# One class of eight PSUM banks, and one ring of SBUF buffers for attention scores, in a one-core NSA and mLSTM step

## The chip, the cores and the metric

The kernel runs on one core of a Trainium2 chip. The metric is the device time of one execution in microseconds (us). The kernel before took 1055.37 us, the median of three runs (1055.33 to 1056.41). TensorE (PE) does the matrix products and writes only to PSUM, which has eight banks of 128 x 512 fp32 values; VectorE (DVE), ScalarE (ACT) and GpSimd (POOL) do the rest, and SyncE (SP) issues nearly all transfers.

## The reference

One inference step through a trunk of two layers, for a prompt of 512 new tokens and for 8 samples of one new token each with 1024 past tokens. Width 1024, fp32.

```python
x <- x + Mixer_i(RMSNorm_i(x));   out = W_out( mix(...) * silu(z) )
# layer 0: native sparse attention, 16 heads of 64 on 4 KV heads
q, kv, win, gates, z = nsa_project(h, w_in)
kc, vc, c_end = compress_branch(kv[:, :, 0:2], pe, w1, b1, w2)   # blocks of 32 rows, stride 16
o = gates[0]*o_c + gates[1]*o_s + gates[2]*o_w                   # compressed, selected, window
# layer 1: mLSTM, 4 heads of 512, chunkwise recurrence
xm, z = split(h @ w_in); c = silu(conv(xm)); q, k from c, v from xm (blocks of 4)
S = (q k^T) * exp(D - mt);  num = S v + decay * q C;  hc = num / max(|den|, exp(-mt))
C = carry_decay * C + k^T (w * v)
out = (rmsnorm(hc) * norm_w + skip * c) * silu(z) @ w_out
```

A final RMSNorm follows. The outputs are both activations, the new cache rows, the window, and the mLSTM states (`C`, `n`, `m` and the convolution's last rows) of the prompt and of the samples.

## The kernel before

Activations stand transposed: features on the 128 partitions, the 520 tokens in two column halves of 260. Every fp32 product is made of three matmuls on parts rounded to the PE's fp32r format: `mm3` (L598) adds whi·xhi, whi·xlo and wlo·xhi into one PSUM tile. Each weight tile is loaded (`wraw`), copied by ACT (`whi`), and subtracted by POOL or DVE (`wlo`); constant strings such as LO_Q choose the engine.

The stages run in this order: norm and the compression of the cache pages, the K/V projection with its tiles turned into natural order (`VNEW`, `VC`, `VT`, `kct`), the query projection (`qr`, `qst`), attention of the prompt (about 300 to 468 us) with the decode work laced in, the output projection, the mLSTM's input projection (`xm`, with the block diagonals `bd` made by DVE), the recurrence with the samples' states `cs` streaming through, the mLSTM's output projection (`uh`, `ul`, added from `mm` into `x` by DVE), and at the end the final norm and the last tiles of the prompt's `C` (`pk`, `kwh`, `kwl`, `pc`, `cpt`, L2739 and on).

All calls to the engines are recorded, and then replayed in orders written out by hand (the tables ORDER and CALLS). So what sets the order on every engine is a list, and it is the same in both kernels. What the pools decide is where a tile lies, and through that which earlier readers an instruction has to wait for. Since all calls are replayed from one line, all instructions have line L504, and the profile is read by the names of the tiles.

PSUM is one pool with four tags: `mm` (2 banks, projections), `s` (3 banks: scores, sums, some transposes), `t` (2 banks, transposes and small products) and `d` (1 bank, decode). A tile of a tag takes the bank of that tag that was let go first in program order. The program has 671 PSUM tiles: 244 of `mm`, 213 of `t`, 180 of `s`, 34 of `d`.

In attention each unit takes score tiles of `s` in PSUM (`s<-KA,qst` and `s<-KB,qst`, two matmuls that add into one tile), DVE writes them with the distance term into an SBUF tile also named `s` (L1471, 7 buffers), ACT takes the exponential, PE turns it, and ACT or DVE copies the turned probabilities to `pt` (L1508, 8 buffers), which the product with V reads. Both SBUF tiles are 128 x 512 fp32.

The decode scores (`dec_qk`, L1163) put a `d` tile into `D["dst"]`, which is read by the add behind it.

Of the kernel before, what the change touches and what calls it, by code (L numbers as in the profile page):

```python
# [9 lines left out]
F32 = mybir.dt.float32  # L10
# [34 lines left out]
SBUFS = 7  # L45
PTB = 8
# [494 lines left out]
def step_kernel(ctx, tc, ap):  # L541
    nc = tc.nc
    R = Rec()
    V, S, G, PE, SP = (Engine(R, n, e) for n, e in (("DVE", nc.vector), ("ACT", nc.scalar), ("POOL", nc.gpsimd),
                                                    ("PE", nc.tensor), ("SP", nc.sync)))
    NE = {"DVE": V, "ACT": S, "POOL": G, "PE": PE, "SP": SP}

    def pool_of(stack, **k):
        return Pool(R, stack.enter_context(tc.tile_pool(**k)), k["bufs"])
# [8 lines left out]
    wp = pool_of(wctx, name="wstream", bufs=2, side="right")  # L558
    ps = pool_of(ctx, name="ps", bufs=1, space=PSUM)

    def bank(tag, bufs, name=None):
        return ps.tile([128, 512], F32, name=name or tag, tag=tag, bufs=bufs)

    def mm_cols(out, lhsT, rhs):
        for c in range(4):
# [1 line left out]
            PE.matmul(out[r], lhsT[:, r], rhs, start=True, stop=True)  # L567

    def mmb():
        return bank("mm", 2)  # L570

    def sb():
        return bank("s", 3)

    def xb():
        return bank("t", 2)

    def db():
        return bank("d", 1)

    cst = const.tile([128, CONSTS.shape[1]], F32, name="cst")
    pt = const.tile([1, 2, 64], I32, name="pt")
# [88 lines left out]
    def rms_close(c, acc, pool):  # L671
        pss = sb()
        PE.matmul(pss[:, :CH], ones, acc, start=True, stop=True)
        rms_factor(pss, pool, rr[c])
# [107 lines left out]
    def cmp_unit(b, c, xp=None):  # L782

        po = sb()
        pw = po[:, 0:256].rearrange("p (h t) -> p h t", h=4)
        raw = cw.tile([128, 2080], F32, name="praw", tag="praw", bufs=3)[:, 0:2048].rearrange("p (g f) -> p g f", g=8)
# [59 lines left out]
    def cmp_second():  # L846

        while second:
            b, c, hs = second.pop(0)
            pk = xb()  # L850
            PE.matmul(pk[:, 0:256], w2[:, c].rearrange("p a d -> p (a d)"), hs.rearrange("p h t -> p (h t)"),
                      start=True, stop=True)
            dst = KC if c == 0 else VT0
            pv = pk[:, 0:256].rearrange("p (a b t) -> p a b t", a=2, b=2)
            for h2 in range(2):
                r = slice(64 * h2, 64 * h2 + 64)
                V.tensor_copy(dst[r, :, b], pv[r, :, h2])
# [4 lines left out]
    def kv_tile(i):  # L862
        w = wkv[i]
        t = cw.tile([128, NTOK], F32, name="kvt", tag="kvt", bufs=3)
        kvt[i] = t
        for c in range(2):
            po = {(0, 1): db, (1, 1): xb, (2, 0): xb}.get((i, c), mmb)()
            for kt in range(8):
                mm3(po[:, :CH], w[0][:, kt], w[1][:, kt], hhi[c][:, kt], hlo[c][:, kt], kt == 0, kt == 7)
                if i == 0:  # L870
                    R.cut()
            V.tensor_mul(t[:, c * CH:(c + 1) * CH], po[:, :CH], rr[c])
        S.dma_start(ap["o_kv"][i], t)
        return t
# [113 lines left out]
    b = 2  # L988
    for i in range(12):
        br, hp = divmod(i, 2)  # L990
# [3 lines left out]
        t = kv_tile(i)  # L994
# [39 lines left out]
    QZ = d1.tile([128, 2, 8, 32], F32, name="QZ")  # L1034
    G.memset(QZ, 0.0)

    PS = d1.tile([128, 1536], F32, name="dPS")
# [54 lines left out]
    D = {}  # L1092
# [70 lines left out]
    def dec_qk(P, u, due):  # L1163

        t, dst = D["dk", u], Tile_("d")

        def run():
            D["dst"] = db()
            kt = D["dk_", u].rearrange("p b (h t) -> p b h t", h=2)
            for par in (1, 0):  # L1170
                for hp in range(2):
                    for cg in (3, 2, 1, 0):
                        b = 2 * cg + par
                        PE.matmul(D["dst"][32 * cg:32 * cg + 32, 0:128], QZ[:, hp, b], kt[:, b, hp],
                                  start=par == 1 and hp == 0, stop=par == 0 and hp == 1)

        def add():
            V.tensor_add(PS[:, u * 128:(u + 1) * 128], PS[:, u * 128:(u + 1) * 128], D["dst"][:, 0:128])
        P.op("PE", 1.3, due, run, r=[t], new=[dst])
        P.op("DVE", 0.2, due + 1.3, add, r=[dst], w=[("PS", u)])  # L1180

# [223 lines left out]
    for k in range(8):  # L1405
# [3 lines left out]
        if k in (3, 5, 7):  # L1409
            u = k // 2 - 1  # L1410
# [9 lines left out]
    at = pool_of(actx, name="att", bufs=3, side="right")  # L1420
# [7 lines left out]
    def att_unit(P, hp, g, i, due):  # L1428
        n = 128 * (i + 1)
        mn, sm = Tile_("mn"), Tile_("sm")  # L1430
        X = {}
# [12 lines left out]
        def part(kind, key):  # L1444
            gk, o = where[key]
            return X[kind, gk][:, o:o + n]
        for gk, ks in enumerate(groups):
            pt_, st = Tile_("s"), Tile_("sx")
            st_.append(st)

            def prod(gk=gk, ks=ks):
                q = qst[hp, g]
                p = X["p", gk] = sb()
                for h2 in sorted({x[1] for x in ks}):
                    kh, brs = 2 * hp + h2, [x[0] for x in ks if x[1] == h2]
                    o = where[brs[0], h2][1]
                    for m, K in enumerate((KA, KB)):
                        if len(brs) == 2:
                            rhs = K[:, kh].rearrange("p (b n) -> p b n", b=2)[:, :, 0:n]
                            out = p[:, o:o + 2 * n].rearrange("p (b n) -> p b n", b=2)  # L1460
                        else:
                            rhs, out = K[:, kh, brs[0] * 512:brs[0] * 512 + n], p[:, o:o + n]
                        PE.matmul(out, q[:, h2, i * 128:(i + 1) * 128], rhs, start=m == 0, stop=m == 1)

            def dist(gk=gk, key=None):
                br, h2 = key
                if key == (0, 0):
                    X["mn"] = at.tile([128, 2, 2], F32, name="mn", tag="mn")
                    X["sm"] = at.tile([128, 2, 2], F32, name="sm", tag="sm")
                if ("s", gk) not in X:  # L1470
                    X["s", gk] = at.tile([128, 512], F32, name="s", tag="s", bufs=SBUFS)  # L1471
                V.tensor_tensor_reduce(part("s", key), part("p", key), D0[:, 384 - 128 * i:512], SLOPES[4 * (2 * hp + h2) + g],
                                       CLAMP, op0=OP.add, op1=OP.min, accum_out=X["mn"][:, h2, br:br + 1])

            def ex(key):
                br, h2 = key
                s = part("s", key)
                S.activation(s, s, AF.Exp, scale=-1.0, bias=X["mn"][:, h2, br:br + 1],
                             accum_out=X["sm"][:, h2, br:br + 1])
            P.op("PE", TA[n], due, prod, r=[D["q", hp, g]], new=[pt_])  # L1480
            for m, key in enumerate(ks):
                f0 = key == (0, 0)
                P.op("DVE", TT[n], due, lambda gk=gk, key=key: dist(gk, key), r=[pt_] + ([] if f0 else [mn]),
                     w=[(mn, key)] + ([(st, key)] if m else []), new=([] if m else [st]) + ([mn, sm] if f0 else []))
                P.op("ACT", TE[n], due, lambda key=key: ex(key), r=[(mn, key)], w=[(st, key), (sm, key)])
# [7 lines left out]
        for gk, ks in enumerate(groups):  # L1493
            h2 = ks[-1][1]
            st, pb_, pt_ = st_[gk], Tile_("s" if h2 else "t"), Tile_("pt")
            pts.append(pt_)

            def scale(key):
                s = part("s", key)
                V.tensor_scalar(s, s, X["sm"][:, key[1], key[0]:key[0] + 1], None, op0=OP.mult)  # L1500

            def tr(gk=gk, m=len(ks) * (i + 1), h2=h2):
                X["pp", gk] = sb() if h2 else xb()
                for j in range(m):
                    PE.transpose(X["pp", gk][:, j * 128:(j + 1) * 128], X["s", gk][:, j * 128:(j + 1) * 128], ident)

            def copy(gk=gk, m=n * len(ks), h2=h2):
                X["pt", gk] = at.tile([128, 512], F32, name="pt", tag="pt", bufs=PTB)  # L1508
                if PTC[2 * i + h2] == "S":
                    S.activation(X["pt", gk][:, 0:m], X["pp", gk][:, 0:m], AF.Copy)  # L1510
                else:
                    V.tensor_copy(X["pt", gk][:, 0:m], X["pp", gk][:, 0:m])
            for key in ks:
                P.op("DVE", TS[n], b_, lambda key=key: scale(key), r=[sm], w=[(st, key)])
            P.op("PE", 0.11 * (i + 1) * len(ks) + 0.02, b_, tr, r=[(st, key) for key in ks], new=[pb_])
            P.op("ACT" if PTC[2 * i + h2] == "S" else "DVE", TC[n], b_, copy, r=[pb_], new=[pt_])
# [22 lines left out]
        u, o = Tile_("u"), Tile_("qo")  # L1539
# [418 lines left out]
    sp = pool_of(sctx, name="st", bufs=1)  # L1958
# [731 lines left out]
    at = 3 + QP0 * 4  # L2690
# [175 lines left out]
```

## Time and profile before

| | before |
|---|---|
| median of 3 runs | 1055.37 us |
| the profiled execution, in all | 1052.93 us |
| its span, first to last instruction | 1051.2 us |
| mean granted TensorE clock | 0.995 |
| DMA, whole span | 197.19 MB, mean 188 GB/s |

How to read it: the profile is of one execution. Busy times of engines overlap; an engine at 97% can still be waited for by others and wait itself. In the page's 40 equal slices of the span PE shows 9 tenths or more in all but three: 7 in the first, and 8 in the 29th (736 to 762 us) and the last. A row of the timeline gives the start, the length, the engine, the line, the operation, what is written and read, partitions x elements, and in brackets how long the engine stood idle just before and what ended that. The busiest single groups are the three matmuls of the projections:

```profile
L504 PE MATMUL mm<-hhi,whi 128*128 128x260 f32 (+1 forms) x952 | 273.9, 288 | 2.2 <-DVE xm L504 1.3
L504 PE MATMUL mm<-hhi,wlo 128*128 128x260 f32 (+1 forms) x952 | 270.4, 284 | 1.0 <-POOL wlo L504 0.7
L504 PE MATMUL mm<-hlo,whi 128*128 128x260 f32 (+1 forms) x952 | 270.3, 284 | 0.0
```

The columns behind the bar are busy us in all, mean ns of one, and the idle time ahead of them with what ended most of it. The first of each three may open a new tile and so wait for a bank; the other two add to it.

### The profile page before, as it was taken

The page shows a single profiled execution, that of the slowest core. Times are in us where ns is not written, and L with a number is a line of the kernel's source. Part 1 is how long each engine was busy: PE and PEld are TensorE (multiplying, and loading weights), DVE is VectorE, ACT ScalarE, POOL GpSimd, SP SyncE. Part 2 cuts the span into 40 slices and gives each one's busy share as a digit, 9 for nine tenths or more (in the row PEclk, how much of TensorE's full clock was granted, in tenths as well). Part 3 has the DMA queues.
Part 4 walks back from the last instruction along what each step waited for, and adds up shares of the span by engine and source line. Part 5 has one row for each costly group of instructions (what it writes and reads, how often), then busy time and mean ns, then how long its engine had stood idle before and what let it go on. Part 6 is the DMA issues. An engine that isn't in the chain of part 4 may idle for free.

```text
span 1051.2 us, 24005 instructions
## 1 busy us (share of the span) xinstructions
PE 1022.5 (97%) x8743; PEld 909.5 (87%) x8743; DVE 787.8 (75%) x1877; ACT 535.0 (51%) x1230; POOL 393.3 (37%) x430
## 2 busy tenths in 40 slices
PE   7999999999999999999999999999899999999998
PEld 6989999899988877779999998898867688787897
DVE  6877764478468887876877675886477998988875
ACT  5253332532467786651444364566555555563533
POOL 1162333434324546462324442342423234434332
PEclk9999999999999999999999999999999999999999
DMA  7664554123435524547435652787789879889543
GB/s 248 202 192 141 156 155 131 36 96 121 144 106 177 141 81 130 153 142 251 142 111 163 203 162 73 243 302 275 259 277 328 273 267 303 295 293 325 161 134 112
DMA packets 124792, 197.19 MB, mean 188 GB/s; under 512 B 16117, under 2 KB 66166, under 8 KB 124418
## 3 DMA queue, kind: packets, MB, share of 16 engines
q1 hardware_dynamic: 118866, 186.37, 54.8%
q10 hardware_dynamic: 5808, 9.28, 2.5%
q8 instruction: 69, 1.13, 0.5%
q14 instruction: 49, 0.40, 0.1%
HBM read 145.89 MB, written 58.10 MB: 194 GB/s over the span
## 4 chain that ended last, share of the span: by engine, by line
PE 83%; DVE 8%; ACT 3%; issue 2%; DMA 1%; SPq 1%; POOL 0%; DVEq 0%; ACTq 0%; POOLq 0%
PE mm L504 51%; PE s L504 18%; PE t L504 10%; PE d L504 5%; ACT s L504 1%; DVE num L504 1%; DVE s L504 1%; DVE cs L504 1%; SPq L504 1%; DMA dk<-in_cache 1%; DVE x L504 1%; DVE qst L504 1%; DMA nw<-in_norms 1%; DVE wlo L504 0%; ACT pt L504 0%
## 5 line engine op out<-in xcount | busy, mean ns | idle before, releaser
L504 PE MATMUL mm<-hhi,whi 128*128 128x260 f32 (+1 forms) x952 | 273.9, 288 | 2.2 <-DVE xm L504 1.3
L504 PE MATMUL mm<-hhi,wlo 128*128 128x260 f32 (+1 forms) x952 | 270.4, 284 | 1.0 <-POOL wlo L504 0.7
L504 PE MATMUL mm<-hlo,whi 128*128 128x260 f32 (+1 forms) x952 | 270.3, 284 | 0.0
L504 PEld LDWEIGHTS mm<-hhi,whi 128*128 128x128 f32 (+1 forms) x952 | 179.2, 188 | 7.2 <-issue 1.7
L504 PEld LDWEIGHTS mm<-hhi,wlo 128*128 128x128 f32 (+1 forms) x952 | 179.1, 188 | 1.6 <-POOL wlo L504 0.9
L504 PEld LDWEIGHTS mm<-hlo,whi 128*128 128x128 f32 (+1 forms) x952 | 178.9, 188 | 0.8 <-DVE hlo L504 0.3
L504 POOL TENSOR_TENSOR wlo<-wraw,whi 128x1024 fp32r<-128x1024 f32 (+2 forms) x55 | 108.8, 1979 | 159.0 <-DVE whi L504 74.8
L504 DVE SCALAR_TENSOR_TENSOR cs<-t,wk,cs 128x512 f32<-128x512 f32 x128 | 88.6, 742 | 6.0 <-ACT cs L504 3.8
L504 ACT ACTIVATE cs<-cs,SBC 128x1024 f32<-128x1024 f32 x64 | 72.0, 1142 | 13.2 <-PE d L504 12.5
L504 POOL TENSOR_SCALAR s<-s,sm 128x128 f32<-128x128 f32 (+3 forms) x63 | 62.8, 1008 | 41.8 <-DVE sm L504 21.1
L504 ACT ACTIVATE s<-s,mn 128x256 f32<-128x256 f32 (+3 forms) x128 | 70.6, 554 | 14.7 <-DVE mn L504 12.7
L504 PE MATMUL s<-phi,w1h 128*128 128x256 f32 (+1 forms) x256 | 77.0, 301 | 0.0
L504 PE MATMUL s<-plo,w1h 128*128 128x256 f32 (+1 forms) x256 | 74.5, 291 | 2.2 <-DVE plo L504 2.0
L504 PE MATMUL s<-phi,w1l 128*128 128x256 f32 (+1 forms) x256 | 74.0, 289 | 0.0
L504 ACT ACTIVATE whi<-wraw 128x1024 fp32r<-128x1024 f32 (+1 forms) x55 | 48.0, 874 | 45.2 <-PE mm L504 34.6
L504 PE MATMUL mm<-uh,whi 128*128 128x260 f32 x224 | 66.5, 297 | 3.6 <-DVE x L504 3.6
L504 DVE CUSTOM_DVE_ANT_0 s<-s,D 128x256 f32<-128x256 f32 (+3 forms) x128 | 57.7, 486 | 10.4 <-PE s L504 7.7
L504 PE MATMUL mm<-uh,wlo 128*128 128x260 f32 x224 | 63.3, 282 | 0.0
L504 PE MATMUL mm<-ul,whi 128*128 128x260 f32 x224 | 63.2, 282 | 0.0
L504 DVE TENSOR_TENSOR wlo<-wraw,whi 128x1024 fp32r<-128x1024 f32 (+1 forms) x47 | 51.9, 1106 | 3.1 <-ACT whi L504 1.8
L504 PEld LDWEIGHTS s<-plo,w1h 128*128 128x128 f32 x256 | 48.5, 189 | 3.9 <-DVE plo L504 2.5
L504 PEld LDWEIGHTS mm<-uh,whi 128*128 128x128 f32 x224 | 42.2, 188 | 9.2 <-DVE x L504 4.5
(479 smaller groups left out, 2650.2 us busy)
## 6 DMA issues: line engine op xcount, KB each, us to landing
cs<-in_state_C SPq DMA_DIRECT2D x64, 512.0 KB, 6.0
o_cs<-cs SPq DMA_DIRECT2D x64, 512.0 KB, 4.8
praw<-in_cache SPq DMA_DIRECT2D x128, 128.0 KB, 3.3
dk<-in_cache SPq DMA_DIRECT2D x128, 128.0 KB, 2.9
wraw<-in_m_in SPq DMA_DIRECT2D x32, 512.0 KB, 4.2
wraw<-in_m_out SPq DMA_DIRECT2D x32, 256.0 KB, 4.4
wraw<-in_w_kv SPq DMA_DIRECT2D x11, 512.0 KB, 4.7
wraw<-in_w_q SPq DMA_DIRECT2D x8, 512.0 KB, 3.6
```

The costliest lines, as they stand in the source:

```text
L504: return f(*[real(x) for x in a], **{n: real(x) for n, x in k.items()})
```

## The change

The four PSUM tags become one tag of eight banks. The SBUF tiles `s` and `pt` of attention share one tag of 7 + 8 = 15 buffers. The decode score tile is kept under a key of its own for each unit, `D["dst", u]`, since several may now be live. No order, no instruction and no constant is changed; on each engine the two programs have the same rows in the same order (PE 5870, DVE 1684, ACT 930, POOL 341 and SP 865 of them), and only the semaphores that they wait for differ.

```diff
     ps = pool_of(ctx, name="ps", bufs=1, space=PSUM)
-    def bank(tag, bufs, name=None):
-        return ps.tile([128, 512], F32, name=name or tag, tag=tag, bufs=bufs)
+    def bank(name):
+        return ps.tile([128, 512], F32, name=name, tag="bank", bufs=8)
...
     def mmb():
-        return bank("mm", 2)
+        return bank("mm")
     def sb():
-        return bank("s", 3)
+        return bank("s")
     def xb():
-        return bank("t", 2)
+        return bank("t")
     def db():
-        return bank("d", 1)
+        return bank("d")
...
         def run():
-            D["dst"] = db()
+            D["dst", u] = db()
...
-                        PE.matmul(D["dst"][32 * cg:32 * cg + 32, 0:128], QZ[:, hp, b], kt[:, b, hp],
+                        PE.matmul(D["dst", u][32 * cg:32 * cg + 32, 0:128], QZ[:, hp, b], kt[:, b, hp],
...
         def add():
-            V.tensor_add(PS[:, u * 128:(u + 1) * 128], PS[:, u * 128:(u + 1) * 128], D["dst"][:, 0:128])
+            V.tensor_add(PS[:, u * 128:(u + 1) * 128], PS[:, u * 128:(u + 1) * 128], D["dst", u][:, 0:128])
...
-                    X["s", gk] = at.tile([128, 512], F32, name="s", tag="s", bufs=SBUFS)
+                    X["s", gk] = at.tile([128, 512], F32, name="s", tag="sp", bufs=SBUFS + PTB)
...
-                X["pt", gk] = at.tile([128, 512], F32, name="pt", tag="pt", bufs=PTB)
+                X["pt", gk] = at.tile([128, 512], F32, name="pt", tag="sp", bufs=SBUFS + PTB)
```

## Prediction, made before the changed kernel was run

> **What bounds the kernel now.** I read three views in this order: the page's busy times and chain, the waits of TensorE, and then the timeline at each place where one of those waits can be a wait for a PSUM bank.
>
> ```profile
> span 1051.2 us, 24005 instructions
> PE 1022.5 (97%) x8743; PEld 909.5 (87%) x8743; DVE 787.8 (75%) x1877; ACT 535.0 (51%) x1230; POOL 393.3 (37%) x430
> PE 83%; DVE 8%; ACT 3%; issue 2%; DMA 1%; SPq 1%; POOL 0%; DVEq 0%; ACTq 0%; POOLq 0%
> ```
>
> TensorE is busy for 97% of the span and holds 83% of the chain that ended last. So most of the time is matmul work which the change leaves alone: no instruction is added, removed or moved on any engine. Only idle time of PE, or the idle time of what PE waits for, can go. The waits of PE, longest sums first (us in total, times, longest one):
>
> ```profile
> PE s L504 <- ACT sq L504: 5.6, 1, 5.6
> PE mm L504 <- DVE x L504: 3.6, 4, 1.5
> PE t L504 <- DVE pr L504: 2.4, 1, 2.4
> PE s L504 <- DVE plo L504: 2.0, 1, 2.0
> ...
> PE t L504 <- DVE dOS L504: 0.4, 1, 0.4
> ```
>
> Each row has to be sorted into one of two kinds. A matmul that reads what the named instruction wrote waits for **data**: `sq`, `pr`, `plo` are read by the next matmul, and no pool of banks changes that. A matmul that writes a bank which the named instruction has just read out waits for a **bank**: `mm` behind DVE `x` (the add of `mm` into `x`), `t` behind a copy of another `t`, `mm` behind `xm`. Those are what the change is about.
>
> **The change part by part.** Before, the classes `mm`, `s`, `t`, `d` own 2, 3, 2 and 1 banks, so a `t` tile takes the bank of the `t` tile two before it. After, a tile takes the bank that was let go longest ago among all eight. The program text gives the count of tiles: 244 `mm`, 213 `t`, 180 `s`, 34 `d`. A bank that had one or two tiles between its uses now mostly has seven. The number of instructions is unchanged, so the cost is nothing in work; what is worth counting is each bank wait and the next date behind it.
>
> *End of the compression stage, 201–206 us.* Timeline rows (start, length, engine, and in brackets the idle time before it and what ended it):
>
> ```profile
> 200.99 0.28 PE L504 MATMUL t<-cst,kct 128*32 128x128 f32 x1 [0.46 <-DVE VNEW L504]
> 202.55 0.28 PE L504 MATMUL t<-cst,kct 128*32 128x128 f32 x1 [0.90 <-ACT VC L504]
> 203.41 1.22 DVE L504 TENSOR_TENSOR wlo<-wraw,whi 128x1024 fp32r<-128x1024 f32 x1
> 204.02 0.33 PE L504 MATMUL t<-cst,VT 128*128 128x128 f32 x1 [0.42 <-ACT VC L504]
> 206.16 0.42 PE L504 MATMUL mm<-hhi,wlo 128*128 128x260 f32 x1
> ```
>
> The three matmuls read `kct` and `VT`, not `VNEW` or `VC`; they wait for the bank. Idle: 0.46 + 0.90 + 0.42 = 1.78. The next date is the matmul at 206.16, which reads the `wlo` that DVE ends at 203.41 + 1.22 = 204.63: PE can come forward by 206.16 − 204.63 = 1.53 before it meets that. DVE's own queue follows PE a little here, so I take **1.3** (ends 0 and 1.53).
>
> *Attention, 300–468 us.* PE has 3 idle us in this window, of which one bank wait shows by name (0.4, `t` behind `dOS`). Shorter ones sit inside the busy time: the first matmul of a score tile writes a new `s` bank, its twin (same shape, same queries) adds to it.
>
> ```profile
> 300.00:468.00 168.00, 164.83 (x1925) 133.46 (x1919) 136.71 (x525) 123.88 (x381) 89.80 (x98) 1.00 0.49 143
> ...
> L504 PE MATMUL s<-KA,qst 128*128 128x512 f32 x48 | 22.0, 459 | 0.3
> L504 PE MATMUL s<-KB,qst 128*128 128x512 f32 x48 | 19.0, 395 | 0.0
> ```
>
> (The first row gives window, span, and busy time of PE, its weight loads, DVE, ACT and POOL, then clock, DMA share and GB/s; the others mean ns of one.) The first of a pair takes 459 − 395 = 64 ns longer, 48 × 64 = 3.1 us; the 48 narrower pairs can add no more than as much, 6.1 in all. That excess is an upper bound, since a first matmul also follows another kind of work. Lower end 0.4. I take **2.4**: 0.4 by name, and two thirds of the 3.1.
>
> ```profile
> DVE s L504 <- PE s L504: 7.7, 14, 1.5
> ACT pt L504 <- PE s L504: 13.4, 14, 2.1
> ```
>
> These rows say what the *SBUF half* of the change is worth. DVE and ACT, in this window, begin `s` and `pt` when PE has made the scores or the transposes, not when a buffer comes free. With seven and eight buffers the oldest one is long done; a shared ring of fifteen gives nothing to wait less for: **0**, ends −0.3 and +0.3 (the 0.3 by the row of `s<-KA`, the only idle time beside it). If the cover went, a `pt` would wait for a transpose that read an old `s`, which is finished by then on the same PE queue.
>
> *Start of the mLSTM projection, 526–530 us.*
>
> ```profile
> 526.42 2.38 POOL L504 TENSOR_TENSOR wlo<-wraw,whi 128x1024 fp32r<-128x1024 f32 x1 [0.70 <-ACT whi L504]
> 526.46 2.49 DVE L504 TENSOR_TENSOR bd<-cst,wc 128x128 f32<-128x128 f32 x1
> 528.87 0.28 DVE L504 TENSOR_TENSOR bd<-cst,wc 128x128 f32<-128x128 f32 x1
> 529.07 0.42 DVE L504 TENSOR_TENSOR xm<-mm,rr 128x260 f32<-128x260 f32 x1
> 529.54 0.39 PE L504 MATMUL mm<-hhi,whi 128*128 128x260 f32 x1 [1.30 <-DVE xm L504]
> ```
>
> PE waits 1.30 for a bank that `xm` reads late, since DVE was held by a `bd` of 2.49 us beside a POOL subtraction that started 0.04 us before it; the next `bd` of the same shape, without POOL beside it, took 0.28. With six more banks the projection goes on: **1.3** (ends 0 and 1.3). [...]
>
> *Output projection and the recurrence, 760–985 us.*
>
> ```profile
> 868.75 0.39 PE L504 MATMUL mm<-uh,whi 128*128 128x260 f32 x1 [0.62 <-DVE x L504]
> 997.48 0.39 PE L504 MATMUL mm<-uh,whi 128*128 128x260 f32 x1 [1.46 <-DVE x L504]
> 1004.82 0.36 PE L504 MATMUL mm<-uh,whi 128*128 128x260 f32 x1 [1.30 <-DVE x L504]
> ```
>
> The row of waits has four such waits, 3.6 us; three are above, the fourth is 3.6 − 0.62 − 1.46 − 1.30 = 0.22 and lies in this window too. Of 0.62 + 0.22 = 0.84 I take **0.6** (ends 0 and 0.84), since the next instructions are data waits with a few tenths to spare.
>
> *The tail of the mLSTM, 985–1011 us.* The two long ones, 1.46 + 1.30 = 2.76, are not worth their length:
>
> ```profile
> 760.00:985.00 225.00, 222.75 (x1565) 167.35 (x1566) 193.91 (x415) 126.82 (x206) 79.82 (x87) 0.99 0.85 286
> 985.00:1011.00 26.00, 23.24 (x190) 21.86 (x189) 24.78 (x62) 9.32 (x21) 8.19 (x7) 1.00 0.59 185
> ```
>
> In the second row DVE is busy 24.78 of 26 us: DVE is the bound there, and PE waits because DVE reads its banks late. A PE that is let go early meets DVE's next product:
>
> ```profile
> 1008.39 0.51 ACT L504 ACTIVATE uh<-HN 128x8 fp32r<-128x8 f32 x4 [1.17 <-DVE HN L504]
> 1009.49 1.28 POOL L504 TENSOR_TENSOR wlo<-wraw,whi 128x512 fp32r<-128x512 f32 x1 [2.24 <-ACT whi L504]
> 1011.25 0.28 PE L504 MATMUL s<-uh,wlo 128*128 128x260 f32 x1
> ```
>
> DVE `HN` lets ACT go on, ACT's next is the `whi` behind which POOL's `wlo` waits, POOL ends at 1009.49 + 1.28 = 1010.77, and PE reads that `wlo` at 1011.25: 0.48 to spare. I take **0.45** (ends 0 and 2.76).
>
> *The end, 1036–1051 us.* From the chain, and two timeline rows:
>
> ```profile
> 1037.01 0.70 DVE kwl L504
> ...
> 1037.76 3.07 PE t L504 x12
> ...
> 1040.85 0.60 ACT cpt L504
> ...
> 1041.50 5.88 PE t L504 x24
> ...
> 1043.27 0.69 DVE L504 TENSOR_TENSOR kwl<-t,kwh 128x512 fp32r<-128x512 f32 x1
> 1044.87 0.39 PE L504 MATMUL t<-vh,kwl 128*128 128x512 f32 x1
> ```
>
> Here all uses are `t` tiles on two banks. PE stands from 1040.83 until `cpt` has left the bank (1041.50, 0.67), and the twelve at 1037.76 stood behind `kwl` reading another (0.70): 1.4 on the path. The later `kwl` ends at 1043.96 and is read at 1044.87, so PE can come forward by 0.91: **0.9** (ends 0 and 1.4). What is late next is that `kwl`.
>
> Sum: 1.3 + 2.4 + 1.3 + 0.6 + 0.45 + 0.9 = 6.95, say **7.0 us**. The profiled execution took 1052.9 in all, 1.7 of it around its span; it is 2.4 below the median of the three runs, 1055.4. The bank waits are the same program in both, so the sum is taken off the median: 1055.4 − 7.0 = **1048.4**. The terms' own uncertainty, halves of most of them, is about 3 either way: 1045.4 to 1051.4.
>
> **The rivals.**
>
> *All of it pays.* Every named bank wait goes in full, and attention gives its upper bound: 1.78 + 6.1 + 1.30 + 3.6 + 0.7 = 13.5, giving 1041.9. For it: each gap is idle PE on a chain that is PE for 83%. Against: the next dates above (1.53, 0.48, 0.91).
>
> *The advance is absorbed.* PE comes out of each stage early and DVE does not, so that the 985–1011 stretch, DVE-bound, ends when it did; only 0.45 + 0.9 = 1.35 remain, 1054.0. For it: DVE's 24.78 of 26. Against it: ahead of that stretch DVE is busy only 193.91 of 225, and waits for PE:
>
> ```profile
> DVE x L504 <- PE mm L504: 7.8, 11, 2.1
> ```
>
> That row is DVE's, in 760–985. An earlier PE brings DVE's adds forward, and with them the start of the stretch. So it needs DVE to be held in that window by something else (its cs transfers, 0.85 DMA share), which I do not see.
>
> *Slower: stretched instructions are dealt anew.* An engine that runs some us earlier meets POOL's subtractions at other places.
>
> ```profile
> 216.15 2.45 DVE L504 SCALAR_TENSOR_TENSOR qst<-qr,qst 64x260 fp32r<-64x260 f32 x1
> ```
>
> One such meeting costs 2.49 − 0.28 = 2.2 by the two `bd` rows, and the row here shows one in the query projection right behind 206 us, where the first 1.3 us are gained and PE uses `wlo` as it is made. DVE's `qr`, `qst` there free the `mm` banks and feed attention. If five more of these fall on the path than now, they cost 11; 11 − 7 = 4 more than before: 1059.4. It turns to slower from four on (4 × 2.2 = 8.8). Against it: banks now give PE seven tiles of room, which hides a DVE that is 2 us late, and a meeting can go as well as come.
>
> *The change does not do what it says.* If the pool took the bank freed last, waits would grow; the program's tiles, though, take the one freed first. For the SBUF half I hold this rival to be true, at 0.
>
> **How the numbers follow.** Forecast (1045.4 to 1051.4) 0.64; all pays 0.10; absorbed 0.14; slower 0.12. About 0.2%, 2.1 us, is what a measurement of this kernel can tell from no change: 1053.3 to 1057.5. Faster: 0.64 + 0.10 = 0.74; same: 0.14; slower: 0.12. The range takes in the first three cases, with half a us or so above the third: 1041.9 to 1055.5.
>
> **What would show it.** Right: no bracket for `VNEW`, `VC`, `xm` at 201–204 and 529; the waits of PE for DVE `x` down from 3.6 to below 1; in the last 10 us no wait for `cpt`; the same rows for `sq`, `pr`, `plo`. The attention step is right if the KA mean of 459 comes near 440 or below. The tail step is right if 985–1011 shows as much DVE work in as long a time, shifted some 5 us earlier, with a new wait of PE for `wlo` at its end. Wrong: a new long PE wait for POOL `wlo` or DVE `qst` in 206–260, DVE busy time above 787.8 by 5 or more, or a shift of PE that shrinks from stage to stage towards 985.

## The result, and the profile after

| | before | changed |
|---|---|---|
| median of 12 runs each | 1055.35 us | 1047.74 us |
| ratio, 95% interval | | 0.9944 [0.9925, 0.9963] |
| the profiled execution, in all | 1052.93 us | 1046.14 us |
| its span | 1051.2 us | 1044.4 us |
| mean granted TensorE clock | 0.995 | 0.998 |

The time predicted was 1048.4. One of the twelve runs before took 5626.69 us, which a median hardly feels. The page of the changed kernel, its span, busy times and chain:

```profile
span 1044.4 us, 23991 instructions
PE 1017.0 (97%) x8743; PEld 908.3 (87%) x8743; DVE 789.8 (76%) x1877; ACT 534.7 (51%) x1230; POOL 392.8 (38%) x430
PE 78%; DVE 10%; ACT 5%; DMA 3%; issue 2%; SPq 1%; POOL 1%; DVEq 0%; ACTq 0%; POOLq 0%
```

The same work, and PE a smaller part of the chain: where PE used to stand for a bank it now more often stands for a product of another engine. The waits of PE of the changed kernel say which:

```profile
PE s L504 <- ACT sq L504: 5.6, 1, 5.6
PE s L504 <- DVE plo L504: 2.8, 2, 2.0
PE t L504 <- DVE pr L504: 2.3, 1, 2.3
PE mm L504 <- POOL wlo L504: 1.6, 2, 0.8
...
PE t L504 <- DVE hs L504: 1.4, 1, 1.4
PE t L504 <- ACT VT L504: 1.0, 1, 1.0
```

The bank waits (`x` 3.6, `VC` 1.3, `xm` 1.3, `cpt` 0.7, `VNEW` 0.5) are gone, all of them. In their place stand `hs`, `VT` and more `wlo`: data.

One thing has to be taken out before the two traces can be laid side by side. Windows of 1 us of the kernel before (window, span, PE busy, granted clock, DMA share, GB/s):

```profile
203.00:204.00 1.00, 0.60 (x2) 1.00 0.00 0
204.00:205.00 1.00, 0.94 (x5) 0.75 0.10 34
205.00:206.00 1.00, 1.00 (x7) 0.50 0.52 120
206.00:207.00 1.00, 1.00 (x6) 0.50 0.76 178
207.00:208.00 1.00, 1.00 (x7) 0.54 0.81 315
208.00:209.00 1.00, 1.00 (x11) 1.00 0.06 25
```

For 3.4 us PE runs at half clock, which costs 1.7 us where PE has work all the while, as here, and less where it would have waited. The trace of before holds three such stretches (204, 651, 760 us; 5.1 us lost), that of after one (755 us; 1.7 lost): half of the 6.8 us between the two spans. So two measures are used below. *At full clock* is a run's time multiplied by its mean granted clock. The *lead* at a place is the start of a matmul in the trace of before less that of the same matmul in the other trace, both reduced by what the half-clock stretches ahead of it cost.

| lead gained in | forecast | changed | changed, again | psum_only | kb_early |
|---|---|---|---|---|---|
| 0 to 187 us | 0 | -1.5 | -2.5 | -3.2 | -0.7 |
| 187 to 206 us | 1.3 | -0.7 | -0.4 | -0.5 | -0.3 |
| 206 to 300 us | 0 | +0.2 | +0.3 | +0.3 | +0.3 |
| 300 to 470 us, attention | 2.4 | +1.2 | +0.6 | +1.4 | +1.4 |
| 470 to 530 us | 1.3 | +1.6 | +1.6 | +1.6 | +1.6 |
| 530 to 660 us | 0 | +0.8 | +0.8 | +0.8 | +0.9 |
| 660 to 985 us | 0.6 | +1.2 | +0.1 | +1.2 | +0.6 |
| 985 to 1011 us | 0.45 | -0.1 | +0.4 | +0.4 | -0.2 |
| 1011 us to the end | 0.9 | +0.6 | +0.6 | +0.6 | +0.6 |

All four columns are kernels with eight shared banks (the last two are described below). Their sums from 187 us on are 4.9, 4.1, 5.9 and 4.8 (the rows are rounded). The first row is no effect of the change: two kernels with the banks of before have -4.2 and -0.7 there (sbuf_only and kb_early_before below). Part of it is a stall near 72 us, which the next section shows; most of the rest is a first matmul up to 0.3 us earlier or later and a wait of 0.6 to 0.9 for `plo` at 44 us, which eight other traces have, kb_early_before among them, and that of before does not. One trace each tells a place to about 1 us where engines collide (attention, 760 to 774 us), and to 0.1 us elsewhere.

### The profile page after: what moved, and what is told of

It is laid out like the page before. It is cut to its first block, busy times and chain, and to the rows that moved or that the text cites. A ratio compares the mean times of both kernels' runs of the same rounds, so it can differ in the third digit from the quotient of the medians.

```text
span 1044.4 us, 23991 instructions
## 1 busy us (share of the span) xinstructions
PE 1017.0 (97%) x8743; PEld 908.3 (87%) x8743; DVE 789.8 (76%) x1877; ACT 534.7 (51%) x1230; POOL 392.8 (38%) x430
## 3 DMA queue, kind: packets, MB, share of 16 engines
q8 instruction: 69, 1.13, 0.4%
## 4 chain that ended last, share of the span: by engine, by line
PE 78%; DVE 10%; ACT 5%; DMA 3%; issue 2%; SPq 1%; POOL 1%; DVEq 0%; ACTq 0%; POOLq 0%
PE mm L504 49%; PE s L504 16%; PE t L504 8%; PE d L504 5%; ACT s L504 2%; DVE cs L504 1%; DVE s L504 1%; DVE num L504 1%; DMA praw<-in_cache 1%; SPq L504 1%; DMA dk<-in_cache 1%; ACT pt L504 1%; DVE plo L504 1%; DVE wlo L504 1%; DVE qst L504 1%
## 5 line engine op out<-in xcount | busy, mean ns | idle before, releaser
L504 PEld LDWEIGHTS s<-phi,w1l 128*128 128x128 f32 x256 | 48.4, 189 | 0.2 <-DVE w1l L504 0.2
```

Source lines behind the costliest of these rows:

```text
L504: return f(*[real(x) for x in a], **{n: real(x) for n, x in k.items()})
```

## The experiments

Each was timed against the kernel before on the same chip, but the four sets ran on four chips. "Full clock" is the mean with its standard error. The kernel before has 1050.0 +- 0.3 in the first set (after_again to mm_with_s), 1048.8 +- 0.2 in the second (t_with_s to tail_short), 1049.8 +- 0.4 in the third (kb_early to warm) and 1048.7 +- 0.5 in the fourth (all_three). Since these differ by up to 1.3 us, the last column sets each run against the before of its own set, and full clock is not compared across sets. The changed kernel, without further edits, has 1045.0 +- 0.3 in 23 runs: those of the result and of after_again.

| run | n | median us | ratio to before, 95% interval | full clock | gain at full clock |
|---|---|---|---|---|---|
| after_again | 11 | 1050.42 | 0.9931 [0.9900, 0.9963] | 1044.8 +- 0.4 | 5.2 +- 0.5 |
| psum_only | 12 | 1052.09 | 0.9956 [0.9929, 0.9984] | 1045.0 +- 0.2 | 5.0 +- 0.4 |
| sbuf_only | 12 | 1057.86 | 1.0014 [0.9988, 1.0039] | 1051.4 +- 0.3 | -1.4 +- 0.4 |
| mm_with_s | 12 | 1055.32 | 0.9987 [0.9960, 1.0014] | 1048.1 +- 0.5 | 2.0 +- 0.6 |
| t_with_s | 12 | 1053.56 | 0.9985 [0.9970, 1.0001] | 1047.9 +- 0.6 | 0.8 +- 0.6 |
| vt_first | 6 | 1046.90 | 0.9925 [0.9898, 0.9951] | 1043.2 +- 0.4 | 5.5 +- 0.5 |
| whi_first | 6 | 1049.04 | 0.9941 [0.9918, 0.9963] | 1043.5 +- 0.5 | 5.2 +- 0.6 |
| tail_short | 7 | 1047.47 | 0.9936 [0.9912, 0.9960] | 1042.7 +- 0.7 | 6.0 +- 0.8 |
| kb_early | 6 | 1046.77 | 0.9923 [0.9898, 0.9949] | 1043.8 +- 0.7 | 6.0 +- 0.8 |
| kb_early_before | 12 | 1052.78 | 0.9981 [0.9963, 0.9999] | 1047.7 +- 0.2 | 2.1 +- 0.4 |
| warm | 12 | 1047.63 | 0.9943 [0.9922, 0.9963] | 1045.7 +- 0.4 | 4.1 +- 0.6 |
| all_three | 6 | 1044.78 | 0.9911 [0.9895, 0.9928] | 1042.9 +- 0.5 | 5.9 +- 0.7 |

**after_again**, no edit.

> The changed kernel again, for the clock. The two profiles differ by 6.8 us of span, but the one of before holds three stretches of about 3.4 us at half clock (about 1.7 us each, 5.1 in all), that of after holds one (1.7). Theory A (bank waits): at equal clock, that is with span x (1 - clock) taken off each run, it is still 4 to 6 us faster than the kernel before. Theory B (clock): at equal clock less than 2.5 us remain, and the rest is that fewer such stretches fall into its runs.

The means of this set are 1056.2 and 1049.6, 6.6 apart, at mean clocks of 0.9941 and 0.9955. At full clock 5.2 remain (1050.0 - 1044.8). Theory A: most of the gain is banks; the other 1.4 us is that the changed kernel's runs had more clock. Whether the change causes that stays open: psum_only, with the same banks, had 0.9940.

**psum_only** and **sbuf_only**, the two halves of the change.

```diff
 # psum_only: the SBUF tags as before
-    X["s", gk] = at.tile([128, 512], F32, name="s", tag="sp", bufs=SBUFS + PTB)
+    X["s", gk] = at.tile([128, 512], F32, name="s", tag="s", bufs=SBUFS)
 ... (and pt likewise)
 # sbuf_only: the bank tags as before, "sp" for s and pt
```

> Eight shared banks, SBUF tags apart as before. Theory A (all of the gain is banks): within 1.0 us of the changed kernel, 1046.7 to 1048.7. Rival (the ring of fifteen SBUF buffers carries part): 2 us or more slower than the changed kernel, most of it in attention (300 to 468 us).

> Banks as before, one ring of fifteen SBUF buffers. Theory A: within 1.0 us of the kernel before, 1054.4 to 1056.4, with all named bank waits in place (xm 1.3, cpt 0.7, x 3.6). Rival: 1053 or less.

By its median psum_only is 4 us above the first set of the changed kernel and 2 above the second, outside the stated 1.0; at full clock it is the same (1045.0, against 1044.8 of after_again in its set). sbuf_only gains nothing, and it has the bank waits of before:

```profile
PE mm L504 <- DVE x L504: 3.5, 4, 1.4
PE t L504 <- ACT VC L504: 1.3, 2, 0.9
PE mm L504 <- DVE xm L504: 1.3, 1, 1.3
PE t L504 <- ACT cpt L504: 0.7, 1, 0.7
```

Its median stands 1.5 us above the range stated, though its lead moves by only 0.1 us from 187 us to the end; its trace has the first row of the table at -4.2. So from 187 us on the ring of fifteen buffers is worth 0, as predicted, and something in the first 100 us differs from run to run. That it is 1.4 us slower than before at full clock is put down to this; no other trace of it was taken, so that is not shown.

**mm_with_s** and **t_with_s**, half of the sharing each.

```diff
-        return ps.tile([128, 512], F32, name=name, tag="bank", bufs=8)
 # mm_with_s
+        tag, bufs = {'mm': ('mm_s', 5), 's': ('mm_s', 5), 't': ('t', 2), 'd': ('d', 1)}[name]
 # t_with_s
+        tag, bufs = {'t': ('t_s', 5), 's': ('t_s', 5), 'mm': ('mm', 2), 'd': ('d', 1)}[name]
 # both
+        return ps.tile([128, 512], F32, name=name, tag=tag, bufs=bufs)
```

> One class of five banks for mm and s; t keeps two of its own, d one. Theory A: the waits of PE for xm (1.3) and x (3.6) go, those at 201 to 204 us, for dOS (0.4) and for cpt (0.7) stay; worth the 529 us step (1.6 by the two profiles), half of attention (0.7) and of the steps at 600 to 985 (1.0): about 3.3 us faster than before at equal clock, against some 5 of the changed kernel. Rival (the t banks carry it): under 1.5 us.

> One class of five banks for t and s; mm keeps two, d one. The times meant are at full clock: each run less its time x (1 - clock); there the kernel before has 1050.0 and the changed one 1045.0 in the runs so far. Theory A (each bank wait is worth what stands at its place): the end (0.75 in the traces so far), 600 to 660 us (0.7) and some of attention (0.5) are gained, 187 to 206 us loses 0.5, the waits for xm (1.3) and x (3.6) stay: 1048 to 1049. Rival (t carries the gain): below 1046.5.

The waits of PE of mm_with_s, then of t_with_s:

```profile
PE t L504 <- ACT VC L504: 1.3, 2, 0.9
PE t L504 <- ACT cpt L504: 0.7, 1, 0.7
PE mm L504 <- DVE x L504: 0.6, 1, 0.6
```

```profile
PE mm L504 <- DVE x L504: 3.5, 4, 1.4
PE mm L504 <- DVE xm L504: 1.3, 1, 1.3
PE t L504 <- DVE hs L504: 1.2, 1, 1.2
PE t L504 <- ACT VT L504: 1.1, 1, 1.1
```

Each half removes its own waits and no other (one `x` of 0.6, at 868 us, outlasts five banks). By the lead, mm_with_s has the 1.6 at 530 us and -0.1 at the end, t_with_s -0.2 at 530 us and 0.7 from 1011 us on: the steps of the table belong to the class named. From 187 us on they sum to 4.3 and 1.4. In time neither is clear of no change by its interval; at full clock 2.0 and 0.8 us are gained. So mm_with_s falls short of the 3.3 expected, though above its rival's 1.5, and in time the halves make 2.8 +- 0.9 of the 5 of the whole, where the leads make 5.7. The traced run of mm_with_s is the fastest of its twelve (1047.8), so its trace may flatter it; why the times of the halves fall short stays open. That each wait belongs to its class is shown, the split of the gain in time is not.

**vt_first**, for the place where the forecast failed.

```diff
 # CALLS0, the pieces at 200 to 206 us
-    853, 829, 670, 839, 830, 831, 840, 671, 873, 750, 841, 874, 875, 877, 842, 876, 751, 857, 868, 843, 861,
-    860, 858, 859, 845, 844, 862, 846, 863, 847,
+    853, 829, 670, 839, 830, 840, 841, 831, 671, 842, 873, 750, 857, 868, 843, 874, 875, 845, 844, 877, 876,
+    751, 861, 860, 858, 859, 862, 846, 863, 847,
```

> The changed kernel with another order at 200 to 206 us: ACT makes the last hsg before the copy of VT, and VT before GT and the VC copies; DVE makes hs before its VC copies. Theory H (with the banks free, PE there waits for hs and VT, which stand behind those copies in ACT's and DVE's queues): the waits for hs (1.4) and VT (1.0) shrink by 0.6 or more together, and PE starts the query projection 0.6 to 1.1 us earlier than in the changed kernel; time at full clock 0.5 to 1.0 lower. Rival (it is the wlo of DVE at 204.6, as the prediction had it): no gain, under 0.2.

A row of before, `hs`, and then the changed kernel there, and vt_first:

```profile
201.96 0.48 DVE L504 SCALAR_TENSOR_TENSOR hs<-s,hcst,hsg 128x252 f32<-128x252 f32 x1
```

```profile
204.72 0.67 PE L504 MATMUL t<-hs,w 128*128 128x256 f32 x2 [1.36 <-DVE hs L504]
206.70 0.76 PE L504 MATMUL t<-cst,VT 128*128 128x128 f32 x5 [0.98 <-ACT VT L504]
```

```profile
203.57 0.67 PE L504 MATMUL t<-hs,w 128*128 128x256 f32 x2 [0.81 <-DVE hs L504]
204.89 0.77 PE L504 MATMUL t<-cst,VT 128*128 128x128 f32 x5 [0.32 <-ACT VT L504]
206.28 0.39 PE L504 MATMUL mm<-hhi,wlo 128*128 128x260 f32 x1 [0.38 <-DVE wlo L504]
```

The two waits shrink from 2.34 to 1.13 and PE reaches the query projection 0.6 us sooner (lead -0.1 in 187 to 206 us against -0.7). Then it meets `wlo`, and at 255 us nothing is left (-0.5 in both). So both theories hold, one behind the other: `hs` and `VT` first, the `wlo` of the prediction next. The 0.5 to 1.0 us expected in time is not shown: vt_first gains 5.5 +- 0.5 in its set and the changed kernel 5.2 +- 0.5 in another.

**whi_first** and **tail_short**, for the stretch at 985 to 1011 us. The changed kernel there:

```profile
992.11 0.39 PE L504 MATMUL mm<-uh,wlo 128*128 128x260 f32 x1 [0.84 <-POOL wlo L504]
995.63 0.39 PE L504 MATMUL mm<-uh,wlo 128*128 128x260 f32 x1 [0.39 <-DVE wlo L504]
997.42 0.39 PE L504 MATMUL mm<-uh,whi 128*128 128x260 f32 x1 [0.34 <-ACT whi L504]
998.22 0.39 PE L504 MATMUL mm<-uh,wlo 128*128 128x260 f32 x1 [0.30 <-DVE wlo L504]
1005.12 0.39 PE L504 MATMUL s<-uh,wlo 128*128 128x260 f32 x1 [0.51 <-POOL wlo L504]
```

Where two bank waits of 2.76 stood, five waits for weights stand, 2.38 in all.

```diff
 # whi_first: ORDER2
-    ... 904, 859, 854, 860, 909, 910, ... 867, 862, 868, 916, 917, ...
+    ... 904, 859, 854, 909, 860, 910, ... 867, 862, 916, 868, 917, ...
 # tail_short: in f_u1 and f_u2
+                m = slice(0, 8 if hd == 3 else T)
-                V.tensor_mul(u, u, X["y"])
+                V.tensor_mul(u[:, m], u[:, m], X["y"][:, m])
...
+                m = slice(0, 8 if hd == 3 else T)
-                E[a].tensor_mul(u, u, X["zs"][:, et])
+                E[a].tensor_mul(u[:, m], u[:, m], X["zs"][:, et, m])
```

> The changed kernel with two whi copies of the output projection ahead of the uh copies that stand before them in ACT's queue (990 and 997 us), where ACT idles 3.4 and 4.6 us for DVE's num. Theory D (DVE's work sets the end of 985 to 1011 us): the wait of PE for POOL wlo at 992 (0.84) and for whi at 997 (0.34) go, but come back behind DVE: at 1011 less than 0.4 us gained. Rival W (the weights' place in ACT's queue sets it): 0.8 us or more gained at 1011.

> The changed kernel; the norm's and the gate's multiplies of the last head work on 8 of 512 columns, so that part of the computation is left out: about 3.6 us less of DVE in 985 to 1003 us. Theory D: PE comes out of 985 to 1011 us 1.2 to 2.4 us earlier than in the changed kernel (its waits for wlo and whi there, 2.4 in all, shrink), and so does the end. Rival W: under 0.4 us.

In whi_first the wait at 992 is gone and 1.0 us is gained by 997 us. Four rows of it show how that is lost again:

```profile
995.74 1.29 POOL L504 TENSOR_TENSOR wlo<-wraw,whi 128x512 fp32r<-128x512 f32 x1 [1.35 <-ACT whi L504]
995.75 1.82 DVE L504 TENSOR_TENSOR num<-num,zs 128x512 f32<-128x512 f32 x1
...
1003.25 0.39 PE L504 MATMUL mm<-uh,wlo 128*128 128x260 f32 x1 [2.17 <-DVE wlo L504]
1005.84 0.39 PE L504 MATMUL mm<-uh,wlo 128*128 128x260 f32 x1 [0.89 <-DVE wlo L504]
```

POOL's subtraction, made earlier, falls beside a multiply of DVE, which takes 1.82 us (the same multiply takes 0.69 in the changed kernel), and all that DVE does behind it is 1.13 us later; 0.4 of that comes back at a multiply that is shorter here (0.69 against 1.11 us), and the next `wlo` of DVE is 0.7 late. In 985 to 1011 us its lead changes by -0.3, that of the changed kernel by -0.1. tail_short, by its one trace, gains 2.8 us there on the changed kernel, somewhat over the 1.2 to 2.4 expected. The windows of the changed kernel and of tail_short (busy time of PE, weight loads, DVE, ACT, POOL):

```profile
985.00:1011.00 26.00, 23.62 (x189) 22.57 (x189) 23.49 (x50) 7.29 (x18) 8.30 (x7) 1.00 0.42 130
```

```profile
985.00:1011.00 26.00, 25.78 (x213) 25.49 (x212) 21.32 (x54) 8.88 (x21) 7.50 (x8) 1.00 0.50 157
```

With 2.2 us less on DVE, PE is busy 25.78 of 26. Theory D holds in the traces: DVE sets the end of this stretch, and a bank given back sooner does not change it. In time, tail_short gains 0.8 +- 0.9 on whi_first, of the same set, which is not clear of nothing.

**kb_early** and **kb_early_before**, for the first 100 us. Rows of after_again, the second trace of the changed kernel:

```profile
70.16 2.37 POOL L504 TENSOR_TENSOR wlo<-wraw,whi 128x1024 fp32r<-128x1024 f32 x1
70.81 5.24 DVE L504 CAST phi<-ones 128x2 fp32r<-128x2 f32 x1
72.46 3.52 POOL L504 MEMSET KB<- 128x4096 f32 x1
76.10 0.69 PE L504 MATMUL s<-phi,w1h 128*128 128x384 f32 x1 [4.88 <-DVE plo L504]
```

A cast of two columns takes 5.24 us: it begins while POOL subtracts a `wlo` (to 72.53) and ends 0.07 us behind POOL's clearing of `KB` (75.98), and PE stands still for 4.88. In the first trace of the same kernel PE's gap was 2.00, in that of before 2.03, in psum_only, sbuf_only and t_with_s 4.88. Where it is about 2.0 this cast begins just ahead of POOL's subtraction (70.64 against 70.69 us in the first trace) and takes 0.15, and only the casts behind it meet the clearing (3.78 and 3.59 us there). So in the two traces of the changed kernel this cast began 0.05 us ahead of the subtraction or 0.65 us behind its start, and which of the two comes falls differently from run to run of one program. The stretch at half clock that follows lasts 6.8 us where the gap was 4.88. The rows show the long cast beside POOL's two instructions; by what means these hold it they do not show.

```diff
 # CALLS0: piece 3, the clearing of KB
-    7, 0, 2, 4, 12, 139, ... 163, 325, 3, 293, 383,
+    7, 0, 2, 4, 3, 12, 139, ... 163, 325, 293, 383,
```

> The changed kernel with POOL's clearing of KB (128 x 4096, 3.5 us) issued at 1 us instead of in the queue at about 72 us. In ten profiles so far PE stands still there for 1.4, 2.0 or 4.9 us, behind a DVE cast that is stretched to 3.1 to 5.2 us beside that clearing, and a stretch at half clock follows in most of them. Theory N (this stall makes the scatter of the runs, of both kernels): the stall goes, the time falls by 2 to 5 us, and the runs lie closer together. Rival (the scatter is the clock's alone): under 1 us.

> The kernel before with the same edit. Theory A (the change is worth about 5.0 us at full clock, whatever the first 100 us do): with the edit in both, the changed kernel is still 4 to 6 us faster at full clock (each run less its time x (1 - clock)). Rival (part of the difference so far comes from which kernel met the long stall how often): under 3.5 us.

The clearing, now at the start, costs nothing that shows, and PE's gap, which now ends with DVE's `phi`, is 1.43 (kb_early):

```profile
1.19 3.54 POOL L504 MEMSET KB<- 128x4096 f32 x1
73.05 0.44 PE L504 MATMUL s<-phi,w1h 128*128 128x384 f32 x1 [1.43 <-DVE phi L504]
```

The mean time of the changed kernel falls from 1049.0 (23 runs, in other sets) to 1046.4, that of before, in one set, from 1055.1 to 1052.7, and the standard deviation of before, at full clock, from 1.7 to 0.75 us. In the changed kernel, with six runs, the scatter did not shrink (1.3 to 1.7). So theory N holds in size, on before in scatter too. As to the worth of the change: with the edit in both, 1047.7 - 1043.8 = 3.9 +- 0.8 at full clock, which lies between the 4 of theory A and the 3.5 of its rival and settles neither; in the medians it is 6.0.

**warm**, for the clock.

```diff
             X["p2"] = xb()
+            for _ in range(2 if hd == 0 else 0):
+                PE.matmul(X["p2"], ones, CT[0][:, 0:512], start=True, stop=True)
```

> The changed kernel with two matmuls of 512 columns put into PE's gap at 753 us, where it waits 2.3 us for DVE's pr; what they write is overwritten. Theory C (a stretch at half clock follows a gap of PE): the stretch that eight of ten profiles show within 10 us behind this gap is gone, the mean clock is higher by 0.001 to 0.002, the mean time 1 to 2 us lower than the changed kernel's 1049.0 of 23 runs. Rival (the stretches come of themselves, as the ones at 390 to 400 and 650 us with no gap ahead): the stretch is there as before.

Windows of the changed kernel, then of warm (the columns as in the prediction; the clock is the number behind the five busy times):

```profile
753.00:755.00 2.00, 0.00 (x0) 0.00 (x0) 1.32 (x7) 0.78 (x3) 0.76 (x3) 1.00 0.83 262
755.00:757.00 2.00, 1.74 (x13) 1.11 (x14) 0.96 (x6) 0.59 (x5) 0.52 (x2) 0.51 0.53 190
757.00:759.00 2.00, 2.00 (x4) 0.67 (x2) 1.86 (x12) 0.61 (x2) 0.00 (x0) 0.64 0.83 147
```

```profile
755.00:757.00 2.00, 2.00 (x8) 0.75 (x5) 1.28 (x8) 1.14 (x4) 0.69 (x3) 1.00 0.96 296
757.00:759.00 2.00, 1.39 (x15) 0.91 (x15) 1.18 (x6) 0.26 (x2) 0.92 (x3) 1.00 0.42 153
759.00:761.00 2.00, 1.71 (x8) 0.55 (x10) 1.68 (x11) 0.94 (x4) 0.41 (x1) 1.00 0.51 152
```

With the gap there, a half-clock stretch follows within 10 us in ten of twelve traces; with the gap filled, in none of two (warm and all_three). The mean clock, 0.9973 +- 0.0004 against 0.9962 +- 0.0008, does not tell by itself. The mean time is 1048.5, 0.5 below the changed kernel's of the other sets and not the 1 to 2 expected; at full clock warm gains 4.1 on its own before, no more than the changed kernel does. Whether the filling itself delays PE was not tested. The traces bear out theory C, and it is worth nothing measurable here.

**all_three**, the edits of vt_first, kb_early and warm on the changed kernel.

> The changed kernel with the three edits together: KB cleared at the start, the other order at 200 to 206 us, two overwritten matmuls in PE's gap at 753 us. If what they took away was there for the stalls that the traces show (1.4 to 4.9 us at 72 us, about 2 at 203 to 206 us, 2.3 at 753 us, each with a stretch at half clock behind it in many runs), the mean clock is 0.998 or more, at full clock the time is 1042.5 to 1044.5, and the median 1044 to 1046.5, below the changed kernel and the one with KB alone (1046.8). If only the clearing of KB counts, it is the same as that one, 1046 to 1047.5.

The traced run has a span of 1041.3 us at a clock of 1.000. The mean clock is 0.9985, the median 1044.78, at full clock 1042.9: inside the ranges for all three edits. It is the lowest median of all, in the set with the lowest median of before too (1053.58); against the changed kernel's own sets (0.9944, 0.9931) the intervals still touch.

## Why the prediction came out, step by step

The time forecast, 1048.4, is within a us of the 1047.74 measured, and that is luck, since two errors cancel in it. The bank waits were worth 4 to 5 us at full clock (5.2 and 5.0 in one set, 3.9 +- 0.8 with the clearing moved in both), or 4.1 to 5.9 by the leads, not 7.0. The rest of the 7.6 is put down to the clock and to the first 100 us, which the prediction did not have as terms: the changed runs of the result had 0.9969 where the before of the other sets had 0.9945, but of the runs before in that set no clock is on record.

- **What is a bank wait and what is data**: right. The rows named as bank waits went, and `sq`, `pr`, and the first `plo` stayed.
- **201 to 206 us, 1.3**: wrong, with about -0.5. The step that failed is "the next date is the matmul at 206.16, which reads the `wlo`". There were two earlier ones, `hs` and `VT`. The first had no bracket in the rows of before: `hs` ended at 202.44 there, inside the bank wait that let PE go on at 202.55; the second lay inside the busy time of the eight transposes that begin at 204.02. Ahead of them 0.6 us is lost at 190 us, behind POOL's `plo`, and won back at 201, where `VNEW` was.
- **Attention, 2.4**: over-sized, 0.6 to 1.4 in the four traces of the table and 0.0 in whi_first, so the term is known to about a us only. The wait behind `dOS` (0.4) went; the two thirds of the 64 ns that the first of a pair takes longer did not. In the trace of after the pair reads so:

```profile
L504 PE MATMUL s<-KA,qst 128*128 128x512 f32 x48 | 21.6, 450 | 0.0
L504 PE MATMUL s<-KB,qst 128*128 128x512 f32 x48 | 19.0, 395 | 0.0
```

The first matmul went from 459 to 450 ns, not to 440: 9 ns x 48 = 0.4 us went with the banks, the other 55 ns have another cause, as the prediction itself had allowed, "a first matmul also follows another kind of work".

- **529 us, 1.3**: right in kind, and somewhat under-sized: 1.6, above its upper end, in all runs in which `mm` had more banks, 0.2 or less in the others.
- **760 to 985 us, 0.6**: 0.1 to 1.2. The waits for `x` went, but kb_early_before, with the banks of before, has 0.6 there too, so the size is not shown. What was left out, 0.7 us at 600 to 660 us, came with the `t` class (0.5 in t_with_s, none in mm_with_s).
- **985 to 1011 us, 0.45**: -0.2 to 0.4. The mechanism is the one given, and tail_short shows it; the wait for POOL's `wlo` at its end (0.51) is there as forecast.
- **The end, 0.9**: 0.6, right in kind. It needs `t`: mm_with_s has -0.1.
- **The SBUF half, 0**: right.
- **The rivals**: "all of it pays" is out by the five new waits of the tail and by 201 to 206 us. "Absorbed" is out: the lead from 529 us reaches the end. Of the slower one, stretched DVE work is dealt anew, but DVE's busy time rose only from 787.8 to 789.8, and whi_first is where it decided.
- **The range**: its upper end, 1055.5, lies 1.5 us above the third case's 1054.0, not the "half a us or so" that the text says.

## What to carry to other kernels

A bank wait in the profile says that PE could have gone on, not how far: look through the data behind it, also those that end inside the wait and those hidden in a row of several matmuls, since the first of them is the new date. A pool with a class for each use wastes banks that one class with the oldest first would lend; here one class paid where an engine was held up for a moment and read its bank late (529 us, a lead of 1.6 us), and next to nothing where that engine is the bound (985 to 1011 us, -0.2 to 0.4). And compare two traces at equal clock, place by place, and times only with runs of the same set, before a difference of half a per cent is explained.

## What was not expected of the hardware

The granted clock fell to half in stretches that cost up to 1.7 us (3.4 us long) or 3.4 us (6.8 us long), by the mean clocks (1.000 to 0.988) from none to about seven of the short ones in a run. In each trace that holds more than one the stretches begin on one grid of 3.413 us; in that of before they begin at 204.50, 651.65 and 760.87 us, 131 and 32 steps apart. Behind the gaps of 4.88 us came the long stretches. Behind those of 2.3 us a stretch came in ten of twelve traces, and the traces say why not in all. The fourteen traces hold 35 stretches, leaving out the last 15 us of each and the start, where the clock is not on record (13.4 us in that of before, 14.4 in the first of the changed kernel). Of these 27 follow a window of the grid in which PE, by its busy rows, stood idle for 1.40 to 3.41 us, 26 of them 1.67 or more. Of some 4100 windows at full clock with no stretch behind them only two had more than 1.61 (1.66 and 1.71). So in these traces about 1.7 us of idle time in a window, half of it, parts the two kinds, in one gap or in two: the gaps of 1.36 and 0.98 at 203 to 207 us left 2.11 in one window of tail_short, with a stretch behind it, and lay in two windows of the first trace of the changed kernel, with none. The two gaps of 2.3 us with no stretch behind them, at 759 us in after_again and at 755 us in tail_short, lay across a border of the grid (0.95 and 1.37, 1.11 and 1.22 us). The other eight stretches, at 390 to 401 us and at 647 to 661 us, had no gap of over 0.7 us in the 10 us ahead of them, and at most 0.19 idle in the window ahead. What starts those stays open.

Clearing a tile of 128 x 4096 on POOL, with the subtraction ahead of it, held a DVE cast for up to 5.24 us (after_again), and with it PE, for 4.88, and then came 6.8 us at half clock. Moved to 1.19 us, where POOL otherwise stood idle for 3.81 us until its first load landed, it cost nothing that shows.
